# Issuing four pairs' products with the tokens already normed ahead of the other half's norm, in a two-layer hybrid block

## The chip, the cores and the metric

The kernel runs on one core of a Trainium2 chip. The metric is the device time of one launch in microseconds (us), as the median of several runs. Five engines work side by side, each strictly in the order in which the program was built: TensorE (PE; its weight loads are shown as PEld), VectorE (DVE), ScalarE (ACT), GpSimd (POOL), and SyncE (SP), which issues nearly all transfers in one queue.

## The reference

The network has two layers over 1024 image tokens and 256 context tokens of width 1024. What the change touches is the end of a layer: the output projection, the second norm and the first product of the MLP. Cut to that:

```python
for l in range(2):
    m  = (silu(c)     @ w_mod[l] + b_mod[l]).reshape(b, 6, 1, 1024)   # modulation
    ...                                                               # three mixers give yx, yc
    xl = xl + m[:, 2] * (yx @ w_out[l])
    hx = modulate(rmsnorm(xl, norm2_g[l]), m[:, 3], m[:, 4])
    xl = xl + m[:, 5] * (relu(hx @ mlp_w1[l]) ** 2 @ mlp_w2[l])
    if l == 0:                                                        # the same for the context xc
        ...
return rmsnorm(xl, final_g)
```

`rmsnorm` divides each token by the root of the mean of its squares, and `modulate(h, shift, scale)` is `h * (1 + scale) + shift`. `mlp_w1` is 1024 x 4096.

## The kernel before, in words

The image tokens are held in two pieces, A and B, of 512 tokens each; the context is piece C, of 256 tokens, and is carried through the MLP of layer 0 alone. Every value that enters a product is split into a high part (written by ACT) and a low part (the rest, written by POOL or DVE), and a product is three matmuls: high by high, low by high, high by low. Names that end in `h` and `l`, or begin with `xh` and `xl`, `whi` and `wlo`, are these parts.

The first product of the MLP (`up`) takes the 4096 columns of w1 in 16 pairs of 128-column blocks. For a pair and the pieces A and B it forms seven products instead of eight, in the manner of Strassen and Winograd: A11·B11, S2·T2, A12·B21, S1·T1, S3·T3, S4·B22 and A22·T4. Each is four slices of the width by three matmuls of 128x512, so 12 matmuls, and a pair has 84. A11, A12, A21 and A22 are quarters of the pair's weights, S1 to S4 sums of them (`up_parts` loads, adds and splits them one pair ahead, in tiles `uA` and `uS`). B11 and B21 are A's normed tokens (`xhA`, `xlA`), which are ready early. T1 to T4 and B22 hold sums of A's and B's normed tokens, which `norm_sums` writes from B's norm; they stay for all 16 pairs. In layer 0 a pair has 48 matmuls of 128x256 for the context too. So of a pair, A11·B11, A12·B21 (they add up to the first block's columns for A) and half of the context's products need nothing of B.

B's norm stands between the output projection (`outproj`, eight blocks of columns, `residual` adding each to B's tokens `xrB`) and the T products. Its chain: ACT squares B's tokens in four tiles, DVE adds the four (L492, L495), PE sums over the width (`cst,sq`), DVE finds the inverse root by Newton steps (`rst`), PE spreads it over the partitions (`cst,rst`), and DVE, ACT and POOL form the T tiles. In DVE and POOL each tile's low part is one instruction, `T2l<-nt,T2h` and the like.

While the pairs of layer 0 run, the modulation of what follows is computed on the side (`mod_part`, a generator that `up` advances twice in a pair, after A12 and after S4): a group of 512 columns is eight loads of 256 KB (`wmod`), accumulated by DVE and ACT/POOL into `macc`, and then turned onto the partitions by PE (`cst,macc`). A group takes two pairs.

Within an engine nothing overtakes: the builder's scheduler has fixed the order of all instructions, PE has six banks for the products in `up`, and loads and stores pass through the one queue of SP. Raw weights, stores of the result `h` and the temporaries of the norm share a ring of 12 slots.

Of the kernel before, what the change touches and what calls it, by code (L numbers as in the profile page):

```python
# [11 lines left out]
AF = mybir.ActivationFunctionType  # L12
# [94 lines left out]
class Net:  # L107
# [333 lines left out]
    def mod_part(self, l, j0, j1):  # L441
# [6 lines left out]
        for g in range(j0, j1, 4):  # L448
            n = 1 if l == 1 and g >= 16 else 2
            acc = self.slot("macc", (n, 512), kind="w")  # L450
            for k in range(8):
# [12 lines left out]
                if k % 2 and k < 7:  # L464
                    yield
# [16 lines left out]
    def rstat(self, p):  # L482

        V = self.V
        ts, n = self.xr[p], LEN[p]
        q, K = n // 128, 1024 // n
        sq = []
        for j, t in enumerate(ts):
            sq.append(self.slot("sq", (K, n), kind="u" if self.share else "x"))
            self.act(sq[j], t, AF.Square)  # L490
            if j % 2:
                V.tensor_tensor(sq[j - 1], sq[j - 1], sq[j], ADD)  # L492
                self.free(sq[j])
        if len(sq) == 4:
            V.tensor_tensor(sq[0], sq[0], sq[2], ADD)  # L495
            self.free(sq[2])
# [46 lines left out]
    def norm_sums(self, l, keep):  # L543
# [6 lines left out]
        for j in range(2):  # L550
            ts = {nm: (self.slot(f"{nm}h", (2, 512), F32R, "a"), self.slot(f"{nm}l", (2, 512), F32R, "a"))
                  for nm in ("T2", "T1", "T3", "B22", "T4")}
            for k in (2 * j, 2 * j + 1):
# [14 lines left out]
                put("T1", o[2], self.P)  # L568
                V.tensor_tensor(o[0], o[1], o[0], SUB)  # L569
                put("T3", o[0], self.P)  # L570
# [4 lines left out]
            for nm, t in ts.items():  # L575
                self.xs.setdefault(nm, []).append(t)
            self.free(keep[j], keep[2 + j], self.xr["B"][j], self.xr["B"][2 + j])
# [946 lines left out]
    def outproj(self, l, p, ys):  # L1524
# [3 lines left out]
        for b in range(8):  # L1528
            self.dense(wv[:, :, b * 128:b * 128 + 128], 128, lambda k, p: (self.block(yh, k), self.block(yl, k)), p, self.residual(b, 16))
        self.free(*yh, *yl)  # L1530
# [18 lines left out]
    def up_parts(self, l, n, x, last):  # L1549
# [12 lines left out]
        put("A11", flat(a11))  # L1562
# [6 lines left out]
        put("A12", flat(a12))  # L1569
# [23 lines left out]
    def up(self, l, last, mod, begin, end):  # L1593
# [31 lines left out]
        xs = self.xs  # L1625
        for n in range(16):
# [23 lines left out]
            def done(w):  # L1650
                self.free(x[w])
                if n == 0 and w == "A11":
                    begin()
# [5 lines left out]
            s1 = tile()  # L1659
            ps = prod("A11", "B11")  # L1660
            ctx(0, "A11", 0)
            self.act(s1, ps)
# [4 lines left out]
            ps = prod("A12", "B21")  # L1667
            ctx(0, "A12", 1)
            third(total(s1, ps, s1), n, 0, 0)
            if not last:  # L1670
                first(cs[0], n, 0, 1024)
# [60 lines left out]
    def mlp(self, l, last):  # L1732
# [12 lines left out]
        def begin():  # L1745
            self.norm_sums(l, self.kept)
            for _ in self.pair:
                pass

        self.up(l, last, mod, begin, parts(0))  # L1750
# [80 lines left out]
    def mixers(self, l, last):  # L1831
# [164 lines left out]
        for _ in range(4):  # L1996
            next(self.pair)
# [107 lines left out]
```

## Time and profile before

| | us |
|---|---|
| median of three runs | 4069.04 |
| the three runs | 4068.16, 4069.04, 4074.85 |
| the profiled execution, its own time | 4074.69 |
| span of the profiled execution | 4072.9 |
| mean granted clock of TensorE | 0.902 of full speed |

The span runs from the first to the last instruction; 1.8 us lie around it. In the rows further below, an engine's busy time is followed by the number of instructions in brackets; "[7.38 <-DVE macc L459]" is the idle time of the engine just before an instruction and what ended it. The granted clock is given as a share: 1.00 is 2.4 GHz, 0.50 is 1.2 GHz. Matmuls overlap, so the cost of one in a row of many is the step from start to start, not its duration.

### The profile page before, as it was taken

To read this page: it belongs to the slowest core of one execution; us is meant where nothing else is said; L and a number is where in the kernel's file an instruction comes from. 1 tells how busy PE (TensorE), PEld (TensorE's weight loads), DVE (VectorE), ACT (ScalarE), POOL (GpSimd) and SP (SyncE) were. 2 spreads that over 40 slices of the span, in tenths; PEclk is the share of its full clock that TensorE was granted. 3 is DMA by queue.
4 is the path that set the end of the run, shared out by engine and by line. 5 is a ranking of instruction groups with operands and counts; after the bars stand their busy time and mean duration, and the time that the engine had idled before them with its cause. 6 is when DMAs were issued, how large, how long until landed. Compare 5 with 4: busy or idle time off the path is not lost. (4 is left out here: it accounts for less than half of the span.)

```text
span 4072.9 us, 61291 instructions
## 1 busy us (share of the span) xinstructions
PE 3616.7 (89%) x23646; PEld 3022.0 (74%) x23646; DVE 2600.5 (64%) x4104; ACT 1397.0 (34%) x2547; POOL 1410.7 (35%) x998
## 2 busy tenths in 40 slices
PE   7998996786788799999999889987698888999998
PEld 4786885675677578888888766876587775888887
DVE  5646877888855755555446644657977658555456
ACT  5434443433334433332111433433343434333120
POOL 1423434332224664432121222114333146553230
PEclk8998887977898799999999999997787898999999
DMA  6334336543374233464331233335344552336221
GB/s 216 115 124 143 115 117 183 163 140 93 110 231 125 87 120 117 130 211 143 100 107 36 87 133 105 104 117 178 99 148 124 161 155 80 109 121 202 88 94 42
DMA packets 502727, 516.37 MB, mean 127 GB/s; under 512 B 34198, under 2 KB 375714, under 8 KB 502434
## 3 DMA queue, kind: packets, MB, share of 16 engines
q1 hardware_dynamic: 502434, 512.45, 40.0%
q8 instruction: 186, 3.05, 0.3%
q14 instruction: 107, 0.88, 0.1%
HBM read 371.39 MB, written 140.94 MB: 126 GB/s over the span
## 5 line engine op out<-in xcount | busy, mean ns | idle before, releaser
L291 POOL TENSOR_TENSOR wlo<-wraw,whi 128x512 fp32r<-128x512 f32 x344 | 489.1, 1446 | 1178.7 <-ACT whi L251 531.2
L251 ACT ACTIVATE whi<-wraw 128x512 fp32r<-128x512 f32 x344 | 205.1, 624 | 340.4 <-PE bank L254 224.0
L254 PE MATMUL bank<-mhB,whi 128*128 128x512 f32 x1024 | 315.9, 390 | 0.0
L254 PE MATMUL bank<-mhA,whi 128*128 128x512 f32 x1024 | 315.2, 389 | 0.0
L1536 DVE SCALAR_TENSOR_TENSOR xrB<-bank,mod,xrB 128x512 f32<-128x512 f32 x176 | 131.6, 749 | 221.7 <-PE bank L254 221.6
L1560 POOL TENSOR_TENSOR uS<-us,uS 128x512 fp32r<-128x512 f32 x128 | 198.8, 1563 | 134.9 <-ACT uS L251 116.9
L1611 DVE TENSOR_TENSOR ms<-bank,ms 128x512 f32<-128x512 f32 x224 | 149.1, 683 | 140.9 <-PE bank L254 108.5
L1560 POOL TENSOR_TENSOR uA<-wraw,uA 128x512 fp32r<-128x512 f32 x112 | 158.9, 1426 | 189.1 <-ACT uA L251 189.1
L254 PEld LDWEIGHTS bank<-mhA,whi 128*128 128x128 f32 x1024 | 192.1, 188 | 39.6
L254 PEld LDWEIGHTS bank<-mhB,whi 128*128 128x128 f32 x1024 | 191.5, 188 | 38.9
L462 POOL TENSOR_TENSOR macc<-macc,wmod 128x512 f32<-128x512 f32 x84 | 130.9, 1559 | 237.1 <-ACT wmod L251 234.9
L1536 DVE SCALAR_TENSOR_TENSOR xrA<-bank,mod,xrA 128x512 f32<-128x512 f32 x176 | 130.0, 746 | 121.0 <-PE bank L254 120.9
L254 PE MATMUL bank<-mhB,wlo 128*128 128x512 f32 x512 | 199.3, 389 | 0.0
L254 PE MATMUL bank<-mhA,wlo 128*128 128x512 f32 x512 | 199.2, 389 | 0.0
L459 DVE SCALAR_TENSOR_TENSOR macc<-wmod,cs,macc 128x512 f32<-128x512 f32 x140 | 138.1, 986 | 81.1 <-DMA wmod<-in_w_mod_dram 53.1
L254 PE MATMUL bank<-xhB,whi 128*128 128x512 f32 (+1 forms) x416 | 165.4, 398 | 13.9 <-ACT ru L251 13.9
L254 PE MATMUL bank<-xhA,whi 128*128 128x512 f32 (+1 forms) x416 | 177.0, 427 | 0.2 <-ACT whi L251 0.2
L254 PE MATMUL bank<-xlA,whi 128*128 128x512 f32 (+1 forms) x416 | 174.5, 421 | 1.3 <-POOL xlA L532 1.0
L695 DVE SCALAR_TENSOR_TENSOR gy<-gu,vt,gy 128x1282 f32<-128x1282 f32 (+1 forms) x96 | 156.2, 1627 | 28.0 <-ACT gy L251 27.3
L254 PE MATMUL bank<-xhA,wlo 128*128 128x512 f32 (+1 forms) x416 | 171.9, 414 | 1.0 <-POOL wlo L291 1.0
L254 PE MATMUL bank<-xhA,uA 128*128 128x512 f32 x512 | 169.6, 393 | 1.4 <-DVE ms L1611 1.4
L254 PE MATMUL bank<-xlB,whi 128*128 128x512 f32 (+1 forms) x416 | 165.0, 397 | 0.0
(511 smaller groups left out, 9869.5 us busy)
## 6 DMA issues: line engine op xcount, KB each, us to landing
wraw<-in_mlp_w_dram SPq DMA_DIRECT2D x256, 256.0 KB
wmod<-in_w_mod_dram SPq DMA_DIRECT2D x192, 256.0 KB
hraw<-h SPq DMA_DIRECT2D x144, 256.0 KB
h<-ms SPq DMA_DIRECT2D x128, 256.0 KB
wraw<-in_w_in_dram SPq DMA_DIRECT2D x100, 256.0 KB
wraw<-in_w_out_dram SPq DMA_DIRECT2D x80, 256.0 KB
rk<-rkb SPq DMA_DIRECT2D x16, 640.0 KB
rt<-rkt SPq DMA_DIRECT2D x16, 640.0 KB
```

The costliest lines, as they stand in the source:

```text
L251: return self.S.activation(out, in_, func, **kw)
L254: return self.nc.tensor.matmul(out, lhsT, rhs, start=start, stop=stop)
L291: self.P.tensor_tensor(lo[:, o + i:o + i + m], raw, h.bitcast(F32), SUB)
L459: V.scalar_tensor_tensor(acc[:, 0], raw, c[0], acc[:, 0], MUL, ADD)
L462: P.tensor_tensor(acc[:, 1], acc[:, 1], raw, ADD)
L695: V.scalar_tensor_tensor(y[:, a:b], u[:, a + t:b + t], w(t), y[:, a:b], MUL, ADD)
L1536: self.V.scalar_tensor_tensor(x, ps, self.lv[self.l]["m"][:, mo + b, i:i + 1], x, MUL, ADD)
L1560: self.P.tensor_tensor(t[:, 1], w, t[:, 0].bitcast(F32), SUB)
L1611: V.tensor_tensor(out, ps, s, ADD)
```

## The change

`ahead(n)` issues, for the pairs 0 to 3 of each layer, A11·B11, A12·B21 and (layer 0) the context's products of the first block, out of separate tiles `whi` and `wlo` of the pair's whole first block, which `wsplit` loads and splits while the output projection runs. The pair itself then leaves them out. Ahead 0 stands before the sum of B's squares, ahead 1 before the spread of the inverse root, aheads 2 and 3 behind the spread. The squares of B and their sum lie within the output projection. The modulation is advanced at other places, so that the turn comes one step after the last accumulation. The low parts of T1 and T3 are written by DVE instead of POOL, and all of B's norm is built before the first S·T product instead of with it.

```diff
...
                 self.free(raw)
-                if k % 2 and k < 7:
+                if k in (2, 5, 7):
                     yield
...
     def rstat(self, p):
 
+        sq = []
+        for j in range(len(self.xr[p])):
+            self.squares(p, j, sq)
+        self.rsum(p, sq)
+
+    def squares(self, p, j, sq):
+
+        t, n = self.xr[p][j], LEN[p]
+        sq.append(self.slot("sq", (1024 // n, n), kind="u" if self.share else "x"))
+        self.act(sq[-1], t, AF.Square)
+        if j:
+            x = sq.pop()
+            self.V.tensor_tensor(sq[0], sq[0], x, ADD)
+            self.free(x)
+
+    def rsum(self, p, sq):
         V = self.V
-        ts, n = self.xr[p], LEN[p]
+        n = LEN[p]
         q, K = n // 128, 1024 // n
-        sq = []
-        for j, t in enumerate(ts):
-            sq.append(self.slot("sq", (K, n), kind="u" if self.share else "x"))
-            self.act(sq[j], t, AF.Square)
-            if j % 2:
-                V.tensor_tensor(sq[j - 1], sq[j - 1], sq[j], ADD)
-                self.free(sq[j])
-        if len(sq) == 4:
-            V.tensor_tensor(sq[0], sq[0], sq[2], ADD)
-            self.free(sq[2])
         st = self.ps()
         for i in range(q):
             for k in range(K):
...
                 V.tensor_tensor(o[2], o[0], a0, SUB)
                 V.tensor_tensor(o[3], o[1], o[2], SUB)
                 put("T2", o[3], V)
-                put("T1", o[2], self.P)
+                put("T1", o[2], V)
                 V.tensor_tensor(o[0], o[1], o[0], SUB)
-                put("T3", o[0], self.P)
+                put("T3", o[0], V)
                 put("B22", o[1], self.P)
                 V.tensor_tensor(o[3], a1, o[3], SUB)
                 put("T4", o[3], V)
                 self.free(*o)
             for nm, t in ts.items():
                 self.xs.setdefault(nm, []).append(t)
+                yield
...
-    def outproj(self, l, p, ys):
+    def outproj(self, l, p, ys, each=lambda b: None):
 
...
         for b in range(8):
             self.dense(wv[:, :, b * 128:b * 128 + 128], 128, lambda k, p: (self.block(yh, k), self.block(yl, k)), p, self.residual(b, 16))
+            each(b)
...
-        put("A11", flat(a11))
+        if n >= self.early:
+            put("A11", flat(a11))
         yield
...
-        put("A12", flat(a12))
+        if n >= self.early:
+            put("A12", flat(a12))
...
-    def up(self, l, last, mod, begin, end):
+    def up(self, l, last, mod, end):
 
 
         V = self.V
...
             self.free(t)
 
         xs = self.xs
+        s1s = []
+
+        def ahead(n):
+
+            hi, lo = self.ahead[n]
+            if n % 2 == 0:
+                s1s.append(self.slot("ms", (2, 512), kind="a"))
+            s = s1s[n // 2][:, n % 2]
+            for h, o in ((0, "B11"), (1, "B21")):
+                ps = self.ps("d")
+                for k in range(4):
+                    rh, rl = xs[o][k // 2]
+                    self.mm3(ps, hi[:, 4 * h + k], lo[:, 4 * h + k], rh[:, k % 2], rl[:, k % 2], k == 0, k == 3)
+                if h == 0:
+                    self.act(s, ps)
+            t = self.slot("mt", (512,), kind="r")
+            third(total(t, ps, s), n, 0, 0)
+            if not last:
+                ps = self.ps("d")[:, :256]
+                for k in range(8):
+                    rh, rl = self.xrhs(k, "C")
+                    self.mm3(ps, hi[:, k], lo[:, k], rh, rl, k == 0, k == 7)
+                first(ps, n, 0, 1024)
+            self.free(hi, lo)
+
+        ahead(0)
+        self.rsum("B", self.sq)
+        ahead(1)
+        sums = self.norm_sums(l, self.kept)
+        for n in range(2, 6):
+            next(sums)
+            if n < self.early:
+                ahead(n)
+        for _ in chain(sums, self.pair):
+            pass
         for n in range(16):
             x, nx = part, {}
             self.part = part = nx
...
             def done(w):
-                self.free(x[w])
-                if n == 0 and w == "A11":
-                    begin()
+                if w in x:
+                    self.free(x[w])
                 next(nxt, None)
                 if n == 15:
                     next(nxt, None)
 
             tile = lambda: self.slot("ms", (512,), kind="r")
-            s1 = tile()
-            ps = prod("A11", "B11")
-            ctx(0, "A11", 0)
-            self.act(s1, ps)
+            ready = n < self.early
+            if ready:
+                s1 = s1s[n // 2][:, n % 2]
+                cs.append(None)
+            else:
+                s1 = tile()
+                ps = prod("A11", "B11")
+                ctx(0, "A11", 0)
+                self.act(s1, ps)
             done("A11")
             ps = prod("S2", "T2")
             done("S2")
             u2 = total(tile(), ps, s1)
-            ps = prod("A12", "B21")
-            ctx(0, "A12", 1)
-            third(total(s1, ps, s1), n, 0, 0)
-            if not last:
-                first(cs[0], n, 0, 1024)
+            if ready:
+                if n % 2:
+                    self.free(s1s[n // 2])
+            else:
+                ps = prod("A12", "B21")
+                ctx(0, "A12", 1)
+                third(total(s1, ps, s1), n, 0, 0)
+                if not last:
+                    first(cs[0], n, 0, 1024)
             done("A12")
             next(mod, None)
             u4 = total(tile(), prod("S1", "T1"), u2)
...
-        def begin():
-            self.norm_sums(l, self.kept)
-            for _ in self.pair:
-                pass
-
-        self.up(l, last, mod, begin, parts(0))
+        self.up(l, last, mod, parts(0))
...
         self.at(1.2)
-        self.outproj(l, "B", yb)
+        self.sq = []
+        self.outproj(l, "B", yb, lambda b: b % 2 and self.squares("B", b // 2, self.sq))
         self.at(1.6)
         self.share = "uw"
+        self.early = 4
+        self.ahead = [self.wsplit(self.w1(l, 2 * n)) for n in range(self.early)]
+        self.save_x(f"xm{l}", "B", False)
         self.raw = [self.up_load(l, fb) for fb in range(2)]
         self.part = {}
         self.pair = self.up_parts(l, 0, self.part, last)
-        for _ in range(4):
+        for _ in range(2):
             next(self.pair)
-        self.save_x(f"xm{l}", "B", False)
-        self.rstat("B")
         self.share = ""
         self.set_rings(d=6, m=2)
         xh, xl = self.xh.pop("A"), self.xl.pop("A")
```

Three places show how it moves instructions. The rows are in program order: number, line, operation, tile written, tiles read, shape; `x8` is eight alike. A `bank` is PSUM, `cst` holds constants. In the trace each matmul one column wide (`cst,sq`, `cst,macc`) shows as two records.

TensorE in layer 1, before, from the last slice of A12·B21 of pair 0 (`uA`) to the first T products:

```order
10314 L254 MATMUL bank_69<-xhA_25660,uA_26003 128x512
10315 L254 MATMUL bank_69<-xlA_25664,uA_26003 128x512
10316 L254 MATMUL bank_73<-cst,sq 128x1 x8
10317 L254 MATMUL bank_69<-xhA_25660,uA_26003 128x512 x2
10318 L254 MATMUL bank_69<-xlA_25664,uA_26003 128x512
10319 L254 MATMUL bank_69<-xhA_25660,uA_26003 128x512
10320 L258 MATMUL bank_73<-cst,rst_3_231 128x128 x4
10321 L254 MATMUL bank_70<-T1h,uS_26013 128x512
10322 L254 MATMUL bank_70<-T1l,uS_26013 128x512
10323 L254 MATMUL bank_68<-T2h,uS_26000 128x512
10324 L254 MATMUL bank_70<-T1h,uS_26013 128x512
10325 L254 MATMUL bank_68<-T2l,uS_26000 128x512
```

TensorE in layer 1, of the change, from the end of ahead 0 (`whi`, `wlo`) to the start of ahead 1:

```order
10348 L254 MATMUL bank_68<-xhA_25678,whi 128x512
10349 L254 MATMUL bank_68<-xlA_25682,whi 128x512
10350 L254 MATMUL bank_68<-xhA_25678,wlo 128x512
10351 L254 MATMUL bank_73<-cst,sq 128x1 x8
10352 L254 MATMUL bank_69<-xhA_25675,whi 128x512
10353 L254 MATMUL bank_69<-xlA_25679,whi 128x512
10354 L254 MATMUL bank_69<-xhA_25675,wlo 128x512
```

and from the end of ahead 1 to the start of ahead 2:

```order
10373 L254 MATMUL bank_70<-xhA_25678,whi 128x512
10374 L254 MATMUL bank_70<-xlA_25682,whi 128x512
10375 L254 MATMUL bank_70<-xhA_25678,wlo 128x512
10376 L258 MATMUL bank_74<-cst,rst_3_231 128x128 x4
10377 L254 MATMUL bank_71<-xhA_25675,whi 128x512
10378 L254 MATMUL bank_71<-xlA_25679,whi 128x512
```

The sum of the squares has moved from within A12·B21 of pair 0 to behind all 24 matmuls of ahead 0, the spread to behind the 24 of ahead 1. Aheads 2 and 3 follow it, 48 matmuls, and only then the S·T products, which come 12 by 12, where before T1 and T2 were mixed slice by slice. In layer 0 each ahead has 24 matmuls of 128x256 for the context as well.

TensorE in layer 0, before, around the turn of a group of the modulation:

```order
4283 L254 MATMUL bank_70<-B22l,uS_11211 128x512
4284 L254 MATMUL bank_70<-B22h,uS_11211 128x512
4285 L254 MATMUL bank_71<-T4h,uA_11260 128x512
4286 L254 MATMUL bank_71<-T4l,uA_11260 128x512
4287 L254 MATMUL bank_71<-T4h,uA_11260 128x512 x2
4288 L254 MATMUL bank_74<-cst,macc 128x1
4289 L254 MATMUL bank_71<-T4l,uA_11260 128x512
4290 L254 MATMUL bank_71<-T4h,uA_11260 128x512 x2
4291 L254 MATMUL bank_71<-T4l,uA_11260 128x512
4292 L254 MATMUL bank_71<-T4h,uA_11260 128x512 x2
4293 L254 MATMUL bank_71<-T4l,uA_11260 128x512
4294 L254 MATMUL bank_74<-cst,macc 128x1 x7
```

and of the change, around the first turn, with S4·B22 of pair 1 ahead of it:

```order
4186 L254 MATMUL bank_70<-B22h,uS_10974 128x512 x2
4187 L254 MATMUL bank_70<-B22l,uS_10974 128x512
4188 L254 MATMUL bank_70<-B22h,uS_10974 128x512
4189 L254 MATMUL bank_74<-cst,macc 128x1 x8
4190 L254 MATMUL bank_71<-T4h,uA_11028 128x512
4191 L254 MATMUL bank_71<-T4l,uA_11028 128x512
```

The eight matmuls of the turn stood within A22·T4, and stand between S4·B22 and A22·T4 now; the last two accumulations, which stood right ahead of them in the code, are issued three products earlier (S1·T1, S3·T3, S4·B22).

VectorE in layer 1, of the change, where B's norm begins:

```order
3299 L1621 TENSOR_TENSOR mt<-bank_70,ms 128x512
3300 L569 SCALAR_TENSOR_TENSOR nt<-xrB_25593,g_1_133,bank_74 128x512
3301 L569 SCALAR_TENSOR_TENSOR nt<-xrB_25595,g_1_133,bank_74 128x512
3302 L569 SCALAR_TENSOR_TENSOR nt<-xrB_25593,g_1_133,bank_74 128x512
3303 L571 TENSOR_TENSOR nt<-nt,keep_25671 128x512
3304 L569 SCALAR_TENSOR_TENSOR nt<-xrB_25595,g_1_133,bank_74 128x512
3305 L572 TENSOR_TENSOR nt<-nt 128x512
3306 L566 TENSOR_TENSOR T1l<-nt,T1h 128x512
3307 L575 TENSOR_TENSOR nt<-nt 128x512
3308 L571 TENSOR_TENSOR nt<-nt,keep_25671 128x512
3309 L566 TENSOR_TENSOR T2l<-nt,T2h 128x512
3310 L566 TENSOR_TENSOR T3l<-nt,T3h 128x512
```

Of these rows the two that write T1l and T3l stood on GpSimd; the first is ahead 0's second product added up, which is new at this place.

## Rows read from the trace of the kernel before

**Rows 1.** Page: engines (busy, share, instructions), and one group (busy us, mean ns | idle before).

```profile
PE 3616.7 (89%) x23646; PEld 3022.0 (74%) x23646; DVE 2600.5 (64%) x4104; ACT 1397.0 (34%) x2547; POOL 1410.7 (35%) x998
...
L1560 POOL TENSOR_TENSOR uS<-us,uS 128x512 fp32r<-128x512 f32 x128 | 198.8, 1563 | 134.9 <-ACT uS L251 116.9
```

**Rows 2.** Windows: length, busy us (instructions) by engine, clock, DMA share, GB/s.

```profile
3300.00:3320.00 20.00, 12.06 (x52) 9.21 (x50) 12.68 (x17) 8.10 (x12) 13.95 (x10) 0.90 1.08 291
...
3360.50:3411.90 51.40, 33.79 (x96) 19.33 (x94) 46.73 (x55) 25.24 (x41) 32.58 (x21) 0.70 0.12 36
...
1315.70:1366.30 50.60, 32.66 (x112) 21.22 (x110) 45.68 (x67) 24.16 (x43) 29.26 (x19) 0.66 0.13 39
...
1402.80:1803.20 400.40, 375.81 (x1934) 323.22 (x1934) 206.84 (x258) 139.08 (x254) 192.75 (x137) 0.96 0.40 130
```

**Rows 3.** Timeline, layer 1: start, us, engine, line, operation [idle before <-releaser].

```profile
3360.05 0.39 PE L254 MATMUL bank<-yl,whi 128*128 128x512 f32 x1
...
3360.28 0.39 PE L254 MATMUL bank<-yh,wlo 128*128 128x512 f32 x1
...
3362.64 1.23 DVE L492 TENSOR_TENSOR sq<-sq 128x1024 f32<-128x1024 f32 x1 [1.19 <-ACT sq L251]
...
3365.18 1.95 PE L254 MATMUL bank<-cst,sq 128*128 128x1 f32 x16
...
3365.87 1.26 POOL L1560 TENSOR_TENSOR uA<-wraw,uA 128x512 fp32r<-128x512 f32 x1 [16.00 <-ACT uA L251]
...
3369.55 0.16 DVE L276 SCALAR_TENSOR_TENSOR rst<-nt,rst 128x4 f32<-128x4 f32 x1
...
3370.54 0.75 DVE L563 SCALAR_TENSOR_TENSOR nt<-xrB,g,bank 128x512 f32<-128x512 f32 x1 [0.82 <-PE bank L258]
```

**Rows 4.** Timeline, layer 1, within B's norm: VectorE and GpSimd.

```profile
3373.50 1.27 POOL L560 TENSOR_TENSOR B22l<-nt,B22h 128x512 fp32r<-128x512 f32 x1 [6.37 <-ACT B22h L251]
...
3374.73 1.72 POOL L560 TENSOR_TENSOR T1l<-nt,T1h 128x512 fp32r<-128x512 f32 x1
...
3377.52 0.68 DVE L560 TENSOR_TENSOR T2l<-nt,T2h 128x512 fp32r<-128x512 f32 x1
...
3384.85 1.76 DVE L560 TENSOR_TENSOR T2l<-nt,T2h 128x512 fp32r<-128x512 f32 x1
```

**Rows 5.** Waits of TensorE over the span: releaser, us, times, longest.

```profile
PE bank L254 <- DVE macc L459: 27.3, 9, 7.4
...
PE bank L254 <- ACT T1h L251: 12.4, 6, 4.2
...
PE bank L254 <- POOL T1l L560: 7.7, 7, 1.3
...
PE bank L254 <- POOL macc L462: 6.0, 4, 2.1
```

**Rows 6.** Timeline, layer 0, at the same place.

```profile
1318.56 0.28 PE L254 MATMUL bank<-xhC,uA 128*128 128x256 f32 x1
...
1318.79 0.40 PE L254 MATMUL bank<-xhC,uA 128*128 128x256 f32 x2
...
1320.40 1.95 PE L254 MATMUL bank<-cst,sq 128*128 128x1 f32 x16
...
1327.10 2.06 DVE L563 SCALAR_TENSOR_TENSOR nt<-xrB,g,bank 128x512 f32<-128x512 f32 x3 [2.17 <-PE bank L258]
```

**Rows 7.** Timeline, layer 0: a turn of the modulation in two pairs.

```profile
1402.82 0.59 PE L254 MATMUL bank<-cst,macc 128*128 128x1 f32 x2 [7.38 <-DVE macc L459]
...
1460.98 2.21 DVE L459 SCALAR_TENSOR_TENSOR macc<-wmod,cs,macc 128x512 f32<-128x512 f32 x2 [1.75 <-DMA wmod<-in_w_mod_dram]
...
1463.25 0.38 PE L254 MATMUL bank<-cst,macc 128*128 128x1 f32 x2 [2.81 <-DVE macc L459]
```

**Rows 8.** Chain that ended last, layer 1: start, us, what.

```profile
3393.11 3.31 DMA wraw<-in_mlp_w_dram
...
3411.91 8.23 PE bank L254 x35
```

## The prediction

> **What bounds the kernel now.** I read the page first, then windows around the two places that the change touches, then the waits of TensorE and single instructions. TensorE works through 89% of the span [rows 1], so what can be won is its idle time and its time at the lower clock. Two places hold much of both.
>
> The first is B's norm between the output projection and the pairs, once in each layer. In layer 1 the last matmul of the projection starts at 3360.28 [rows 3], and TensorE runs without a gap only from 3411.91 [rows 8]. In the 51.4 us between, it issued 96 records, of which 16 are the sum of squares and 4 the spread: 76 products, at a mean granted clock of 0.70, while DVE was busy for 46.7 us [rows 2]. A product costs 0.23 us from start to start at full clock (3360.05 to 3360.28, [rows 3]), so 76 need 17.3 us. The other 34 us are waits for T1h, T1l and their like [rows 5] and half speed. Layer 0 looks alike from 1315.7 to 1366.3: 112 records less 22 small ones make 90 products, 24 of them the context's narrow ones, at clock 0.66 [rows 2]. A narrow one costs 0.12 us (a row of two lasts 0.40, a row of one 0.28, [rows 6]).
>
> The second place is the turning of the modulation in the pairs of layer 0. TensorE waits 27.3 us for DVE's macc and 6.0 us for POOL's over the span [rows 5]: 7.38 us at the first turn of the stage, 2.81 at the second [rows 7]. There are eight turns, each two pairs behind the one before, so the stretch from the first to the eighth, 1402.8 to 1803.2, is 14 pairs. Their work at full clock is 14 x (84 x 0.227 + 48 x 0.12) = 347 us, and the 86 records left over [rows 2] at 0.12 make 10. The stretch took 400.4 us at clock 0.96 [rows 2]: 43 us went there. With the wait of the first turn itself the modulation costs 51 us. The page's 89% hides this, since TensorE at half speed counts as busy.
>
> **The change, part by part.** Times are sums against the profiled execution, 4074.7 us.
>
> *Aheads.* The number of products is the same. Added are, per layer, eight loads of 256 KB (A11 and A12 are still loaded for the sums); eight casts on ACT and eight on POOL take the place of those of A11 and A12 of four pairs. They lie within the projection: POOL is idle for 16.00 us just before it ends [rows 3], and eight casts at 1.27 us alone [rows 4] take 10; the loads, 2 MB, have a queue that moved 291 GB/s a little earlier [rows 2], so 7 us. I cost them at nothing; without that cover ahead 0 would start late by up to 10.
>
> *B's norm in layer 1.* One DVE add of 1.23 us [rows 3] no longer follows the last residual. Instead the sum of squares stands behind ahead 0, which ends at 3360.5 + 24 x 0.227 = 3365.9. Before, the sum began at 3365.18, and the inverse root was done 4.5 us later [rows 3], so it is done at 3370.4 now. The spread stands behind ahead 1: 3365.9 + 1.9 for the sum + 5.4 = 3373.2, and DVE's norm starts at 3374.1, which is 3.6 us later than 3370.54 [rows 3]. What this delays is covered: TensorE has aheads 2 and 3 until 3384.9.
>
> Then the length of DVE's part decides. Before it took some 40 us (3370.54 to 3410.7) with 32 operations for the norm and a handful of others. Now it has 40, as T1's and T3's low parts come over from POOL. Such an operation takes 0.68 us while POOL rests and 1.76 us while it works, and POOL's 1.27 becomes 1.72 [rows 4]. POOL keeps only the four low parts of B22 in this stretch. Lower end: 40 at 0.65 make 26 us. Upper end: the old 40 us plus eight at 0.68 make 45. I take 30 (40 at 0.65, four of them a microsecond longer), near the lower end because POOL's part falls from twelve to four. So DVE is through at 3404 and TensorE runs on from 3404.5, with the 96 products of the aheads and about 12 T products done: 108, against 76 at 3411.9. The gain is 7.4 + 32 x 0.227 = 14.7 us. I take off 2 for products at half speed between 3385 and 3404, which leaves **13 us**; the ends of DVE's part give 17 and -2.
>
> *B's norm in layer 0.* An ahead is 24 x 0.227 + 24 x 0.12 = 8.3 us. The sum starts at 1315.7 + 8.3 = 1324.0 (before 1320.40), the spread is over at 1335, and DVE starts at 1335.2, or 8.1 us later than 1327.10 [rows 6]. With 30 us it ends at 1365.2, about where TensorE got going before (1366.3), but 108 wide and 96 narrow products are done then, against 66 and 24: 0.8 + 42 x 0.227 + 72 x 0.12 = 19.0 us, less 2 for the clock, **17 us** (ends 21 and 2).
>
> *Short pairs.* Pairs 0 to 3 now need 60 wide products, 13.6 us in layer 1 and 60 wide and 24 narrow ones, 16.5 us, in layer 0. POOL has 6 casts there and 3.5 additions of the modulation in a pair of layer 0. At 1.56 us, its mean beside DVE [rows 1], that is 14.8 us: under 16.5, but barely. DVE has 16.5 operations; 9.5 slowed ones at 1.76 and 7 at 0.68 would make 21.5 us. Ends: 0 and 4 x 5 = 20 us lost. If instead the two only ever work in turn, the times alone add up: 9.5 x 1.27 + 10.5 (weight sums, squares, modulation) x 0.65 = 18.9 us in a pair, 2.4 over, 10 us in four. I take 3, nearer to nothing, since six banks let the totals lag and the mean of 1.56 already holds what POOL waited. The Trainium skill, "SBUF — State Buffer", section "Who interferes with whom", says that a DVE instruction with two SBUF inputs and a GpSimd instruction that reads SBUF hold one port in turn, the later one waiting for the whole of the earlier; by that rule the 10 would be lost. The trace bears it out in part: the two slowed operations of [rows 4] take 1.76 and 1.72 us where 0.68 and 1.27 add up to 1.95.
>
> *Modulation.* The last two accumulations now come 36 wide products, 8.2 us, ahead of the turn. The waits of 7.38 and 2.81 us [rows 7] and all later ones are shorter than that. If they go, so does the half speed behind them, for nothing else in the stretch idles TensorE for long. Ends: all 51, or 20, if the accumulations, which begin when a load has landed (DVE waited 1.75 us for one, [rows 7]), stay late in half of the turns. I take **43**, since two turns fall into short pairs.
>
> **Sum.** 13 + 17 - 3 + 43 = 70: 4074.7 - 70 = 4004.7 us. The profiled execution lies 5.7 us above the median and beside the highest of three runs; a median of later runs may lie anywhere between, so I say 4003.
>
> **Rivals.**
> 1. *The modulation's wait changes queues.* DVE reaches the early accumulations before their load has landed and stands there, with the pair's totals behind it; banks stay full and TensorE waits again. DVE's wait for the load in [rows 7] speaks for it, the six banks (13.6 us of products) against. It leaves 20 of the 51: 4075 - 27 - 20 = 4028.
> 2. *DVE becomes the bound.* Upper ends of the norms (-2 and 2) and 12 lost in short pairs: 4075 + 12 - 43 = 4044. For it: DVE was busy 46.7 of 51.4 us [rows 2]. Against: most of its slow operations stood beside POOL's twelve.
> 3. *DVE and POOL work only in turn* in the short pairs of layer 0: 10 lost instead of 3, 4012. For it: the slowed operations of [rows 4]; against: DVE and POOL were busy for 46.7 and 32.6 us of the 51.4 in layer 1's norm [rows 2], 79 us together, so they did overlap, if slowed.
> 4. *Slower: the queue.* The raw weights of pairs 1 to 3 stand in SP's queue behind stores of the aheads' results. A raw load was on the chain once, 3.31 us [rows 8]. A short pair moves 1 MB of w1, 0.79 to 0.92 MB of h and in layer 0 1 MB of w_mod: 1.79 and 2.92 MB, 18.8 MB for the eight pairs, in 120 us of TensorE's time. The stretch of full pairs ran at 130 GB/s [rows 2]; at that rate the eight need 145 us and 25 of the 70 are lost. From 95 GB/s down the whole gain and 8 us more are gone: 198 us. At 85 GB/s the time is 4075 - 70 + 102 = 4107. Against it: 291 GB/s were reached [rows 2], and DMA stood at a 0.40 share in the full pairs, so 130 was what was asked for, not what was possible.
>
> **How the numbers follow.** Forecast, 3980 to 4010: 0.54. Rival 3, to 4018: 0.12. Rival 1, to 4036: 0.14. Rival 2, to 4052: 0.12. Rival 4: 0.04. Something near no change through several of these: 0.04. The range reaches from all bounds on the good side, 4069 - 89 = 3980, to the middle of rival 2, 4045, and leaves out about 0.15. Measurements of this kernel tell a change from none at about 0.2%, 8 us: faster 0.93, same 0.03, slower 0.04.
>
> **What would show it.** Of the changed kernel: TensorE continuous from the end of the projection for about 24 us in layer 1 and 36 us in layer 0 at clock 1.00; the first operation of DVE's norm 13.6 us after the projection's end in layer 1 (10.0 before) and 19.5 in layer 0 (11.4); its last low part 30 us later; no wait for macc over 1 us between the turns; two turns apart by about 51 us in full pairs (the mean before is 400.4 / 7 = 57); POOL below 90% in the short pairs of layer 0. Wrong would be a gap of several us ahead of a product of S2 or S1 in pairs 0 to 3 (rivals 2 to 4, told apart by what ends it), DVE idle for a w_mod load with totals behind it (rival 1), or ahead 0 waiting for its weights.

## The result, and the profile after

| | before | after |
|---|---|---|
| median, us | 4070.53 (4 runs, 4068.16 to 4074.85) | 4004.84 (4 runs, 4003.24 to 4007.97) |
| ratio | | 0.9838, 95% interval 0.9821 to 0.9855 |
| span of the profiled execution, us | 4072.9 | 4002.8 |

The change makes the kernel faster by 66 us; 4003 was forecast. How much of that is the forecast's own sum is another matter. It is seen when both profiled executions are cut at the same instructions (the last product of the pairs is the last T product; in layer 0 the context's last matmuls come behind it):

| stretch | before, us | after, us |
|---|---|---|
| start to the output projection of layer 0 | 1155.0 | 1163.6 |
| projection of layer 0, to B's last product | 160.4 | 163.4 |
| from there to the last product of the pairs, layer 0 | 493.3 | 445.4 |
| second product of the MLP, norm and input projection, to the mixers of layer 1 | 526.3 | 524.1 |
| mixers of layer 1, to the projection | 903.2 | 885.8 |
| projection of layer 1 | 122.1 | 119.2 |
| from there to the last product of the pairs, layer 1 | 339.2 | 329.6 |
| rest | 373.5 | 371.4 |

The two stages of pairs lost 47.9 and 9.6 us. The mixers of layer 1 lost 17.4 and the first stretch gained 8.6; on both nothing was forecast.

Windows of the changed kernel (length, busy us and instructions of PE, PEld, DVE, ACT, POOL, granted clock, DMA share, GB/s): from the end of the projection to where TensorE runs on, in layer 1 and in layer 0 (against the second and third row of [rows 2]); the short pairs of layer 0; and the two stages of pairs whole.

```profile
3301.99:3348.99 47.00, 31.39 (x131) 23.13 (x129) 38.75 (x65) 25.25 (x43) 8.47 (x5) 0.81 0.23 75
1327.30:1380.42 53.12, 42.42 (x229) 34.87 (x227) 40.62 (x80) 29.39 (x56) 10.50 (x6) 0.89 0.25 80
1380.42:1462.00 81.58, 70.08 (x319) 59.23 (x320) 58.96 (x61) 30.24 (x52) 61.81 (x40) 0.86 0.41 124
1327.30:1772.70 445.40, 423.19 (x2207) 363.26 (x2206) 276.26 (x362) 175.87 (x319) 238.27 (x159) 0.95 0.42 134
3301.80:3631.40 329.60, 313.99 (x1365) 256.96 (x1364) 206.24 (x282) 116.77 (x199) 173.12 (x117) 0.96 0.40 127
```

In layer 1 the stretch under the norm is 47.0 us where it was 51.4, with 131 - 20 = 111 products where there were 76, and POOL has 5 operations where it had 21. In layer 0 it is 53.1 us where it was 50.6, with 229 - 22 = 207 products (111 wide, 96 narrow) for 90. The third row is the surprise: in the short pairs TensorE is busy for 70.1 of 81.6 us, at clock 0.86.

The timeline of layer 1 in the changed kernel, with what ended the idle time in brackets; it answers to [rows 3] and [rows 4].

```profile
3292.15 0.98 DVE L1574 TENSOR_TENSOR us<-wraw 128x512 f32<-128x512 f32 x1 [5.53 <-DMA wraw<-in_mlp_w_dram]
...
3307.43 1.84 PE L254 MATMUL bank<-cst,sq 128*128 128x1 f32 x16
3314.71 0.60 PE L258 MATMUL bank<-cst,rst 128*128 128x128 f32 x4
3315.68 2.05 DVE L569 SCALAR_TENSOR_TENSOR nt<-xrB,g,bank 128x512 f32<-128x512 f32 x3
...
3320.05 1.39 POOL L566 TENSOR_TENSOR B22l<-nt,B22h 128x512 fp32r<-128x512 f32 x1 [19.32 <-ACT B22h L251]
3320.21 1.78 DVE L575 TENSOR_TENSOR nt<-nt 128x512 f32<-128x512 f32 x1
...
3336.91 0.79 PE L254 MATMUL bank<-T2h,uS 128*128 128x512 f32 x1 [8.21 <-ACT T2h L251]
...
3345.38 0.61 ACT L251 ACTIVATE uS<-us 128x512 fp32r<-128x512 f32 x1
...
3345.93 0.68 DVE L566 TENSOR_TENSOR T4l<-nt,T4h 128x512 fp32r<-128x512 f32 x1
3346.04 0.79 PE L254 MATMUL bank<-T1h,uS 128*128 128x512 f32 x1 [1.16 <-ACT uS L251]
3346.07 2.87 POOL L1568 TENSOR_TENSOR uS<-us,uS 128x512 fp32r<-128x512 f32 x1 [7.22 <-DVE T3l L566]
...
3348.99 1.22 PE L254 MATMUL bank<-T1h,uS 128*128 128x512 f32 x2 [1.73 <-POOL uS L1568]
```

DVE's norm starts 13.7 us after the projection's end (3301.99) and its last low part ends 30.9 us later. The aheads end at 3326, and TensorE then waits for T2's second half, 8.21 us in one piece. Last comes S1: its high part, written by ACT behind the norm's T4h and done at 3345.99, then its low part, which POOL starts at 3346.07; the trace ends POOL's wait by DVE's T3l, done at 3346.01. The sum from which both are made was there long before (the row of 3292.15), but the program issues S1's two parts behind all of B's norm.

The waits of TensorE for macc in the pairs of layer 0 of the changed kernel (us, times, longest), against the first and last row of [rows 5], and the second turn on SP, DVE and TensorE:

```profile
PE bank L254 <- DVE macc L459: 7.2, 2, 4.9
PE bank L254 <- POOL macc L462: 4.1, 2, 2.2
```

```profile
1445.04 5.17 SPq L264 DMA_DIRECT2D h<-ms  x3
1452.26 0.33 SPq L261 DMA_DIRECT2D wmod<-in_w_mod_dram  x1
...
1455.24 0.75 DVE L459 SCALAR_TENSOR_TENSOR macc<-wmod,cs,macc 128x512 f32<-128x512 f32 x1 [5.38 <-DMA wmod<-in_w_mod_dram]
...
1456.05 0.58 PE L254 MATMUL bank<-cst,macc 128*128 128x1 f32 x2 [4.88 <-DVE macc L459]
```

Both turns that wait stand in short pairs. DVE stands 5.38 us for the last load of the group, which SP issues only at 1452.26. Three stores of the pair's results stand ahead of it in the queue, but they were issued by 1450.21. What ends the load's wait is GpSimd, which shows in SP's waits between 1376 and 1462 (us, times, longest), and in GpSimd's rows ahead of this turn and of the first one:

```profile
SPq L261 <- POOL macc L462: 22.8, 11, 5.1
SPq L261 <- POOL uA L1568: 9.8, 3, 6.6
```

```profile
1398.53 5.14 POOL L462 TENSOR_TENSOR macc<-macc,wmod 128x512 f32<-128x512 f32 x3
...
1403.70 0.34 SPq L261 DMA_DIRECT2D wmod<-in_w_mod_dram  x1
...
1407.52 0.75 DVE L459 SCALAR_TENSOR_TENSOR macc<-wmod,cs,macc 128x512 f32<-128x512 f32 x1 [3.30 <-DMA wmod<-in_w_mod_dram]
```

```profile
1450.97 1.26 POOL L1568 TENSOR_TENSOR uA<-wraw,uA 128x512 fp32r<-128x512 f32 x1
```

GpSimd's operations end at 1403.67 and 1452.23, and each of the two loads leaves 0.03 us later. All loads and stores here share the ring of 12 slots, and a slot is free when its last reader is done: for a `wmod` or a `wraw` tile that is often GpSimd.

### The profile page after: what moved, and what is told of

Same layout as the page of the kernel before. It is cut to its first block, busy times and chain, and to the rows that moved or that the text cites. A ratio compares the mean times of both kernels' runs of the same rounds, so it can differ in the third digit from the quotient of the medians.

```text
span 4002.8 us, 61327 instructions
## 1 busy us (share of the span) xinstructions
PE 3587.2 (90%) x23646; PEld 3007.7 (75%) x23646; DVE 2574.5 (64%) x4120; ACT 1394.9 (35%) x2547; POOL 1381.4 (35%) x982
## 4 chain that ended last, share of the span: by engine, by line
PE 54%; DVE 11%; DMA 3%; issue 2%; POOL 2%; ACT 2%; SPq 0%; DVEq 0%; ACTq 0%; POOLq 0%
PE bank L254 53%; DVE iD L835 1%; DVE iE L836 1%; DVE iD L829 1%; DMA wmod<-in_w_mod_dram 1%; DMA wraw<-in_mlp_w_dram 0%; DMA yin<-y 0%; POOL macc L462 0%; PE bank L1195 0%; POOL wlo L291 0%; PE bank L258 0%; POOL ras L1153 0%; DVE nt L275 0%; DVE iF L837 0%; DVE rsv L1327 0%
## 5 line engine op out<-in xcount | busy, mean ns | idle before, releaser
L291 POOL TENSOR_TENSOR wlo<-wraw,whi 128x512 fp32r<-128x512 f32 x360 | 503.1, 1420 | 1251.4 <-ACT whi L251 554.6
L251 ACT ACTIVATE whi<-wraw 128x512 fp32r<-128x512 f32 x360 | 214.2, 623 | 369.1 <-PE bank L254 165.8
L254 PE MATMUL bank<-xhA,whi 128*128 128x512 f32 (+1 forms) x480 | 203.6, 425 | 0.0
L254 PE MATMUL bank<-xlA,whi 128*128 128x512 f32 (+1 forms) x480 | 199.6, 417 | 0.3 <-POOL xlA L538 0.3
L254 PE MATMUL bank<-xhA,wlo 128*128 128x512 f32 (+1 forms) x480 | 199.0, 416 | 0.6 <-POOL wlo L291 0.6
L254 PE MATMUL bank<-xhB,whi 128*128 128x512 f32 (+1 forms) x416 | 165.5, 398 | 13.7 <-ACT ru L251 13.7
L254 PE MATMUL bank<-xhB,wlo 128*128 128x512 f32 (+1 forms) x416 | 164.3, 395 | 0.0
L1568 POOL TENSOR_TENSOR uA<-wraw,uA 128x512 fp32r<-128x512 f32 x96 | 140.4, 1472 | 60.3 <-ACT uA L251 57.5
```

The costliest lines, as they stand in the source:

```text
L251: return self.S.activation(out, in_, func, **kw)
L254: return self.nc.tensor.matmul(out, lhsT, rhs, start=start, stop=stop)
L291: self.P.tensor_tensor(lo[:, o + i:o + i + m], raw, h.bitcast(F32), SUB)
L1568: self.P.tensor_tensor(t[:, 1], w, t[:, 0].bitcast(F32), SUB)
```

## The experiments

Each row "stages" below gives the two stretches of pairs, layer 0 and layer 1 (493.3 and 339.2 before, 445.4 and 329.6 after). They are the measure for single steps: whole runs of one kernel lay up to 27 us apart (below), these stretches within 1 us (445.4 and 445.9, 329.6 and 329.6 in the two profiles of the change).

**The later turning alone**, on the kernel before.

```diff
-                if k % 2 and k < 7:
+                if k in (2, 5, 7):
```

> The kernel before with the later turning of the modulation alone. Theory (the modulation's waits and the half speed behind them cost 51 us of the pairs of layer 0, and the turn three products later removes most): the stage of pairs in layer 0 goes from 493 to about 453 us, TensorE waits for macc under 3 us there, the time is about 4030. Rival (the wait moves into VectorE's queue and comes back through the banks): 20 us only, 4050. Second question: in the changed kernel the mixers of layer 0 took 9 us longer and those of layer 1 17 us less, with the same order of instructions in layer 1. If the later turning did that, layer 0 reaches its output projection at 1163 us here, not at 1155.

Median 4024.11 (4014.07 to 4031.75), ratio 0.9871 (0.9845 to 0.9897). Stages 448.3 and 339.2. The window of its pairs in layer 0, and its waits there:

```profile
1315.70:1764.00 448.30, 424.99 (x2208) 361.35 (x2207) 286.17 (x353) 175.97 (x324) 253.50 (x172) 0.95 0.42 132
```

```profile
PE bank L254 <- DVE macc L459: 2.4, 1, 2.4
PE bank L254 <- POOL macc L462: 1.8, 1, 1.8
```

The same 2208 records take 45.0 us less, at clock 0.95 instead of 0.92; 32 us of waits for macc in that stretch (26.0 and 6.0) became 4.2, of which all is at the first turn. The rival falls. The first stretch took 1157.6 us, the mixers of layer 1 895.2: no sign that the turning matters to either.

**All but the later turning.**

```diff
-                if k in (2, 5, 7):
+                if k % 2 and k < 7:
```

> The changed kernel with the modulation turned where it was. Theory (the parts add up): the stage of pairs in layer 0 goes from 446 to about 486 us, layer 1 stays at 330 from its projection to its last pair, the time is about 4045. Rival (the aheads alone had also shortened the modulation's waits, since VectorE is through with B's norm sooner): 4025. If the later turning made the mixers of layer 0 slower, the projection there begins at 1155 here, not at 1163.

Median 4048.57 (4045.26 to 4050.56), ratio 0.9932 (0.9911 to 0.9953). Stages 484.6 and 329.5. The aheads alone are worth 8.7 us in layer 0 and 9.7 in layer 1. In layer 0 the two parts alone make 45.0 + 8.7 = 53.7, together 47.9: 6 us are lost to their meeting.

**Two pairs ahead instead of four.**

```diff
-        self.early = 4
+        self.early = 2
```

> The changed kernel with two pairs' products ahead instead of four. Theory (what lies under B's norm is what is gained): 48 wide products less under the norm, 10.9 us in layer 1 and 16.6 in layer 0 with the context's, less some 3 us since only two pairs are short: layer 1 goes from 330 to 340 us, layer 0 from 446 to 460, the time is about 4029. Rival (short pairs give as much back as the aheads bring, VectorE and GpSimd being the bound there): 4012 or less.

Median 4027.12 (4019.34 to 4036.25), ratio 0.9881 (0.9853 to 0.9909). Stages 461.0 and 338.9. The theory's 460 and 340 hold: in layer 1 two aheads bring nothing against the kernel before. There TensorE issued 97 records in the 51.4 us behind the projection, and 96 before the change ([rows 2]): the old order, which mixed products of T1 and T2, had as much work beside the norm.

**T1's and T3's low parts back on GpSimd.**

```diff
-                put("T1", o[2], V)
+                put("T1", o[2], self.P)
...
-                put("T3", o[0], V)
+                put("T3", o[0], self.P)
```

> The changed kernel with the low parts of T1 and T3 written by GpSimd, as before. Theory (VectorE's operations are slowed by each operation of GpSimd beside them, 0.68 to 1.76 us, so the move shortens B's norm): VectorE's part of the norm takes 36 to 40 us instead of 31 although it has eight operations less, 5 to 9 us in each layer, the time is 4015 to 4023. Rival (the move only costs VectorE eight operations, about 5 us a layer): 3995.

Median 4018.53 (4005.43 to 4027.94), ratio 0.9867 (0.9840 to 0.9893). Stages 449.8 and 330.5. VectorE's part of the norm took 41.2 us in layer 0 (31.3 in the change) and 34.3 in layer 1 (30.9). Two of its operations beside GpSimd:

```profile
1345.74 1.78 DVE L578 TENSOR_TENSOR nt<-keep,nt 128x512 f32<-128x512 f32 x1
1347.44 1.77 DVE L575 TENSOR_TENSOR nt<-nt 128x512 f32<-128x512 f32 x1
```

The mechanism is as stated: 15 operations of over 1 us in layer 0 where the change has 5. The price is smaller than expected, 4.4 and 0.9 us. In layer 1 TensorE runs on at 3349.42, before the last low part is done at 3349.99, so the late parts are not the ones that it needs. In layer 0 the norm is 9.9 us longer and the stage 4.4; why it is not more stays open.

**The squares behind the projection.**

```diff
-        self.outproj(l, "B", yb, lambda b: b % 2 and self.squares("B", b // 2, self.sq))
+        self.outproj(l, "B", yb)
...
+        for j in range(4):
+            self.squares("B", j, self.sq)
```

> The changed kernel with the squares of B issued behind the whole output projection again, as before. Theory (their sum on TensorE stands behind ahead 0, which ends 5.4 us after the projection, so the last square and two additions, some 4.9 us, are hidden): VectorE's norm starts 13.9 us after the projection's last matmul in layer 1 and 19.7 in layer 0, as in the changed kernel, and both stages of pairs keep their 330 and 446 us. Rival (the squares on the side of the projection are part of what made it 2 to 3 us shorter in layer 1, or of the start of the norm): 1 to 5 us in a layer.

Median 4007.12 (3992.89 to 4020.03), ratio 0.9824 (0.9790 to 0.9858). Stages 444.3 and 329.6; VectorE's norm starts at 3320.84, 13.9 us after the projection's last product at 3306.9, as in the change. Moving the squares is worth nothing behind an ahead.

**Six pairs ahead in layer 1.**

```diff
-        self.early = 4
+        self.early = 6 if l else 4
```

> The changed kernel with six pairs' products ahead in layer 1 alone. Theory (TensorE is idle for about 15 us of the 18 before it runs on, waiting for the T parts, and two more aheads, 10.9 us, fit in): layer 1 goes from 330 to about 320 us from its projection to its last pair, layer 0 stays. Rival (VectorE's norm grows by the two additions, and the two more short pairs are bound by VectorE and GpSimd): 325 or more.

Median 4001.23 (3994.98 to 4007.76), ratio 0.9810 (0.9784 to 0.9837). Stages 445.7 and 321.8: 7.8 us less in layer 1. By the ratio this can't be told from the change, by the stage it can. VectorE's part of the norm grew with it, from 30.9 to 36.8 us (3324.68 to 3361.48), as the rival had it in part. Of the some 15 us of idle time that it aimed at, one piece of over 1 us is left:

```profile
3357.44 0.79 PE L254 MATMUL bank<-B22h,uS 128*128 128x512 f32 x1 [9.14 <-ACT uS L251]
```

**The modulation out of the short pairs, three steps a pair afterwards.**

```diff
             done("A12")
-            next(mod, None)
+            if n >= 4:
+                next(mod, None)
...
             done("S3")
+            if 4 <= n < 12:
+                next(mod, None)
...
             done("S4")
-            next(mod, None)
+            if n >= 4:
+                next(mod, None)
```

> The changed kernel with the modulation started in pair 4 and advanced three times a pair up to pair 11, so that the four short pairs of layer 0 have none of it. Theory (what the aheads of layer 0 gained under the norm, about 16 us, is given back in the short pairs because the modulation's loads, additions and turns crowd them: 11.3 us of waits for macc and the half speed behind them): the stage of pairs in layer 0 goes from 446 to about 432 us. Rival (the short pairs are bound by the pair's own work on GpSimd and VectorE, or by the w1 loads): 441 or more, with waits for uS or uA in place of macc.

Median 4016.85 (4013.73 to 4029.44), ratio 0.9854 (0.9827 to 0.9882). Stages 450.2 and 329.1. The short pairs ran without a gap of 0.3 us up to the first turn, so they are bound by TensorE once the modulation is out of them. But with three steps in a pair a turn can stand one product behind its last accumulation, and the waits came back there:

```profile
1549.82 0.38 PE L254 MATMUL bank<-cst,macc 128*128 128x1 f32 x2 [3.94 <-DVE macc L459]
1554.03 2.29 PE L254 MATMUL bank<-cst,macc 128*128 128x1 f32 x10 [3.83 <-POOL macc L462]
...
1667.15 1.87 PE L254 MATMUL bank<-cst,macc 128*128 128x1 f32 x8 [5.97 <-DVE macc L459]
```

The total refutes the 432, and the cause named for it stands; the next but one kernel tells the two apart.

**The same with six pairs ahead in both layers.**

```diff
-        self.early = 4
+        self.early = 6
```

> As the kernel with the modulation started in pair 4, and with six pairs' products ahead in both layers. Theory: the gains add up. Layer 1 at about 320 us, layer 0 at about 420 (two more aheads, 16.6 us, of which the idle time before the first S·T products run on takes some 12). Rival (six short pairs are too many for GpSimd and the queue): layer 0 no better than with four.

Median 4014.26 (3998.96 to 4019.44), ratio 0.9836 (0.9799 to 0.9873). Stages 458.8 and 319.5: layer 1 as expected, layer 0 worse, with the same crowded turns.

**The modulation out of the short pairs, two steps a pair afterwards.** As the kernel with three steps a pair, but without the step at S3, and with two steps instead of one at the context's piece in the second product. Of the edit the diff shows what is new against that kernel.

```diff
                     if len(fbs) == 4:
-                        next(mod, None)
+                        for _ in range(2 if p == "C" else 1):
+                            next(mod, None)
```

> The changed kernel with the modulation started in pair 4 and advanced twice a pair as in the change, so that a turn stays three products behind its last accumulation; the steps that no longer fit are taken in the second product of the MLP, where a sixth more steps stand. Theory (the four short pairs of layer 0 lose their time to the modulation alone; with three steps a pair the turns were too close to their accumulations): no wait for macc over 1 us, the stage of pairs in layer 0 at about 432 us instead of 446, the second product not longer. Rival (full pairs of layer 0 need those waits anyway, or the steps that are put off make the second product longer): 440 or more in all.

Median 3990.77 (3986.96 to 3991.36), ratio 0.9785 (0.9772 to 0.9799). Stages 426.3 and 329.6. Its pairs of layer 0, and its short pairs, which took 70.1 busy of 81.6 us in the change:

```profile
1323.20:1749.50 426.30, 414.31 (x2191) 356.22 (x2190) 260.18 (x343) 173.42 (x317) 233.22 (x159) 0.98 0.41 130
1376.63:1460.00 83.37, 83.36 (x413) 71.17 (x414) 49.35 (x62) 28.79 (x53) 48.88 (x35) 0.97 0.37 117
```

In about the same time TensorE issues 413 records for 319. The stage lost 19.1 us; two of its eight turns (the last ones, of 8 records each) have moved into the second product, 16 records or 2 us, and the stretch after it took 526.3 for 524.1. So some 17 us of the change's own gain had been given back to the modulation in the short pairs.

**That, with six pairs ahead in both layers.**

```diff
-        self.early = 4
+        self.early = 6
```

> As the one with the modulation started in pair 4, two steps a pair, and with six pairs' products ahead in both layers. Theory: layer 0 at about 428 us from its projection to its last pair, layer 1 at 320 to 322 as with six ahead there alone; together some 25 us less than the changed kernel, about 3982. Rival (six short pairs in a row outrun GpSimd and the queue in layer 0): layer 0 at 435 or more.

Median 3986.43 (3977.97 to 3996.86), ratio 0.9777 (0.9759 to 0.9795). Stages 430.6 and 319.6. Pair 4 is short now and has modulation: one turn waits 5.1 us for VectorE and 1.9 for GpSimd. In layer 0 six aheads are no better than four.

**The change once more**, without an edit.

> The changed kernel once more, beside the others on the same chip. Theory (the mixers' time, which no edit touches in layer 1, varies by 20 us from execution to execution with the granted clock): the stages of pairs come out at 446 and 330 us again within 1 us, and the mixers of layer 1 anywhere between 886 and 905. Rival (the change itself made them shorter): 886 again, within 3 us.

Median 4010.69 (4005.75 to 4018.84), ratio 0.9838 (0.9822 to 0.9854). Its mixers of layer 1, and below, those of the first profile of the same program:

```profile
2293.70:3196.80 903.10, 767.12 (x6622) 644.46 (x6620) 620.38 (x1094) 331.94 (x655) 260.41 (x193) 0.85 0.41 127
```

```profile
2296.70:3182.50 885.80, 748.26 (x6620) 627.32 (x6619) 618.62 (x1094) 330.89 (x655) 260.44 (x193) 0.87 0.42 129
```

Stages 445.9 and 329.6 again. The mixers took 903.1, as before the change (903.2). The rival, 886 again, falls.

**The best value of each stage.** Modulation as in the kernel with two steps a pair, four pairs ahead in layer 0, six in layer 1.

```diff
-        self.early = 4
+        self.early = 6 if l else 4
```

> The modulation started in pair 4, two steps a pair, four pairs' products ahead in layer 0 and six in layer 1: the best value of each stage so far. Theory (the stages don't act on each other): 426 us in layer 0 and 320 to 322 in layer 1, some 29 us less than the changed kernel, a median near 3981 with runs from 3970 to 3992 as the mixers fall. Rival: one of the two stages is longer by over 3 us than in the kernel that it is taken from.

Median 3986.69 (3970.52 to 3996.25), ratio 0.9789 (0.9762 to 0.9816). Stages:

```profile
1326.10:1751.90 425.80, 414.31 (x2191) 356.05 (x2190) 263.54 (x345) 173.02 (x317) 234.97 (x159) 0.98 0.41 130
3283.30:3605.20 321.90, 311.70 (x1366) 256.13 (x1365) 210.03 (x283) 115.85 (x197) 173.84 (x117) 0.98 0.41 131
```

The stages don't act on each other: 27 us less than the change in the pairs. The median is 6 us above the theory's, with its mixers anywhere in their 20 us.

## Why the prediction was right, and where it was not

*The total.* 4003 against 4004.84, but not by its sum alone, and in part by luck. Of the 70.1 us between the two profiled executions the pairs brought 57.5. The projections (3.0 longer, 2.9 shorter) cancel, the stretches behind the pairs brought 2.2 and 2.1, and the rest, 17.4 - 8.6 = 8.8 us, came from the mixers. The change run again, with its mixers at 903.1, shows that the edit doesn't fix their time. Over all runs on record, 36 of the kernel before and 8 of the change, the means are 4075.4 and 4008.4: 67 us, some 5 more than the pairs, the projections and the stretches behind the pairs explain (61.7). There is one profile of the kernel before, so where these 5 come from stays open.

*Aheads at nothing.* Right for layer 1. In layer 0 the projection took 161 to 164 us with the aheads' loads and casts in it and 158 to 160 without, so some 3 us may be theirs; no experiment took them out alone.

*Start of the norm.* Right: 13.7 us forecast as 13.6, and 19.4 (1346.71 less 1327.3) forecast as 19.5. The squares, costed at nothing, are worth nothing.

*DVE's 30 us.* Right: 30.9 and 31.3. That GpSimd's rest is what shortens it is shown by putting the low parts back.

*13 us in layer 1.* Measured 9.6. The step that was short is the end: TensorE was to run on 0.5 us behind the last low part, and it was 2.4, as S1's parts stand behind the norm and the low one took 2.87 us, where such a cast takes 1.27 alone. With DVE 0.9 longer and its start 0.1 later that makes the 47.0 us in place of 44. The two gaps of TensorE in front of S1's parts, 1.16 and 1.73 us, stand in layer 0 as well (1.17 and 1.73); no run issued these parts ahead of the norm.

*17 us in layer 0, 3 given back, 43 for the modulation.* The 17 had come in when TensorE ran on: 45 more wide and 72 more narrow products in 2.5 us more, 10.2 + 8.6 - 2.5 = 16.3. The turning alone, without short pairs, brought 45.0 of the 51; within the change it brought 39.2 (484.6 - 445.4), where 43 was forecast. The term that failed is the short pairs: 3 us for them and 8 left over for turns in them, 11 in all, where about 17 were lost. Of TensorE's 11.5 us without work there, 11.3 are waits for macc at two turns. That the forecast had as the sign of its first rival: VectorE stands for a w_mod load, and TensorE for the turn. The load is late because it waits for a slot that GpSimd has to free. GpSimd's three macc ahead of the first turn took 5.14 us, where three at 1.27 would take 3.8, so the slowing of the third rival may have a part; no run separates the two, since taking the modulation out of the short pairs takes both away. The pair's own casts and totals, of which the second and third rival were afraid, cost nothing by themselves, since the short pairs run gapless without the modulation. The prediction had counted their operations and the queue's bytes and not the slot for which a load waits.

*The bound of 0.2%.* Too fine. Four to nine runs of one kernel spread over 4 to 27 us here, so a change of 8 us is seen in a stage and not in a median of four.

## What to carry to other kernels

Work without a dependence, placed under a serial stretch, gains what it fills beyond what the old order had there; but what it leaves behind are shorter rounds, and side work that is paced by the round, not by time, then crowds them. Count for each load of such side work what it waits for in the short round: the queue ahead of it, and the engine that must free its buffer. Where a stage that no edit touches moves as much as the change, cut the executions at the same instructions and compare the stretches.

## What the runs showed of the hardware

TensorE, VectorE and GpSimd work through the mixers of layer 1 in the same order before and after, and no experiment edits them. Over the fourteen profiles they took 885.6 to 904.6 us. What differs is the granted clock, 0.87 in the shortest and 0.85 in the longest. One place, some 10 us behind the same matmul (at 3054.25 before and 3009.69 after), in windows of the kernel before and of the changed one:

```profile
3064.00:3074.00 10.00, 10.00 (x64) 8.63 (x66) 4.99 (x13) 2.72 (x7) 1.13 (x3) 0.50 0.16 55
```

```profile
3019.50:3029.50 10.00, 8.42 (x111) 6.99 (x109) 9.21 (x25) 4.16 (x12) 1.11 (x2) 1.00 0.27 76
```

In 10 us TensorE issues 64 records at half speed, without rest, and 111 at full speed with rests. The rows don't tell why the same work is granted full speed in one execution and half in another; that stays open.

In the timeline of layer 1 above, GpSimd's operation starts at 3320.05 and ends at 3321.44, and VectorE's, begun at 3320.21, ends at 3321.99, 0.55 us after it, which is about its whole length alone, 0.68. GpSimd's was not much longer than alone, 1.39 for 1.27. The Trainium skill, "SBUF — State Buffer", section "Who interferes with whom", says that a VectorE instruction with two inputs in SBUF contends with a GpSimd instruction that reads SBUF, and that their shared ports are an exclusive lock. The trace agrees there: the later one waited for the whole of the earlier. The cast of 2.87 us, beside VectorE operations that kept their 0.68, shows the other side.
